# The first two matrices of a feed-forward layer: seven products of quarters in place of eight

## The chip, the cores and the metric

The kernel runs on one core of a Trainium2 chip. The metric is the time of one execution in device microseconds (us). Runs of the kernel before gave a median of 1726.57 us, from 1723.56 to 1729.68 (three runs).

## The reference

Two layers work on 256 context tokens and 256 latent tokens of width 1024. Layer 0 mixes with a recurrence and grouped attention and then runs a dense feed-forward layer (D_FF = 2816) over all 512 tokens; layer 1 mixes with a long convolution and latent attention and then runs a mixture of experts. The change lies in the dense feed-forward layer alone:

```python
def swiglu(h, w1, w3, w2):
    return (jax.nn.silu(h @ w1) * (h @ w3)) @ w2
...
def channel_mix(h):
    if even:
        return swiglu(h, ffn_w1[j], ffn_w3[j], ffn_w2[j])
    return moe_swiglu(h, moe_router[j], moe_w1[j], moe_w3[j], moe_w2[j])
...
xl = xl + mod_l[5] * channel_mix(modulate(rms_norm(xl, norm2_g[layer]), mod_l[3], mod_l[4]))
if need_ctx:
    xc = xc + mod_c[5] * channel_mix(modulate(rms_norm(xc, norm2_g[layer]), mod_c[3], mod_c[4]))
```

All of it is float32.

## The kernel before, in words

**Precision.** A float32 operand is held as two F32R tiles, `hi` (a rounded copy, by ScalarE) and `lo` (what the rounding left out, by a VectorE subtract). One product is `mm3` (L576): three matmuls, hi·hi, hi·lo and lo·hi, with a 128x128 piece of a weight stationary and the activations moving.

**Activations of the feed-forward layer.** The normed input stands transposed in eight tiles `h[k]`, each 128 channels by 512 tokens (tag `hhi`, `hlo`); columns 0 to 255 are the context, 256 to 511 the latents. `norm_pair` (L568) makes one `h[k]`: ACT writes hi, DVE writes lo, in two halves.

**Weights.** `Stream` (`ws`, L186 to L293) brings all weight matrices in their order of use: SP starts a DMA of 1 MB into one of two `raw` tiles (NR = 2), ACT copies it in two pieces of 128x1024 to `whi` (L260) and DVE subtracts to `wlo` (L273). `take()` gives the next block and splits one block ahead (LA = 1).

**The loops.** `FFN_PARTS` (L44) cuts the 22 column tiles of D_FF into parts of 8, 8 and 6. In a part, each iteration `b` (a "pair" below) does a w1 block and a w3 block of 256 columns: 2 blocks x 2 column tiles x 8 contraction tiles x 3 = 96 matmuls with 512 moving columns. ACT takes the silu from PSUM to `fs` (L1120), DVE multiplies by the w3 result (L1124), and `hilo` (L555 to L557) splits the product into `ah` (ACT) and `al` (DVE). Then four blocks of w2 (L1132 on) multiply the part's activations into the residual stream (`resid`, DVE, L1058). The first pair of the first part is different: each `h[k]` is made just ahead of its own matmuls.

```python
            else:
                bh, bl = take()
                p1 = [bank(), bank()]
                for m in range(2):
                    c = slice(m * 128, m * 128 + 128)
                    for k in range(KD):
                        mm3(p1[m], bh[:, k, c], bl[:, k, c], h[k][0], h[k][1], k == 0, k == KD - 1)
                bh, bl = take()
                p3 = bank2()
```

**Modulation.** `tick()` (L448) does one 128-row piece of the modulation matrices of a later stage: four small matmuls (L458) on a piece `rm` that came by DMA into a ring, here of 2 + 6 slots (L1054). Ticks are sprinkled through the loops; `tick_end` (L465) closes each eighth one.

**What sets the order.** From the norm to the end of the first pair the order on PE, DVE and ACT is the program's (`manual_schedule`, L1088 to `order.close()`, L1107). Elsewhere a scheduler orders each engine's instructions at build time from its own estimates; every engine then runs its list in that order. GpSimd (POOL) has no work in the feed-forward layer.

Of the kernel before, what the change touches and what calls it, by code (L numbers as in the profile page):

```python
# [138 lines left out]
def program(tc, a, out):  # L139
# [46 lines left out]
    class Stream:  # L186
# [389 lines left out]
    def mm3(p, wh, wl, xh, xl, first, last):  # L576
        TE.matmul(p, wh, xh, start=first, stop=False)  # L577
        TE.matmul(p, wh, xl, start=False, stop=False)  # L578
        TE.matmul(p, wl, xh, start=False, stop=last)  # L579
# [510 lines left out]
    pb = norm_last(0, 0, p, pn, (1, 3))  # L1090
    first = [take(0), take(0)]
    h = []
    for m0, mn in FFN_PARTS:
        act = []
        for b in range(mn // 2):
            if m0 + b == 0:
                p1, p3 = [bank(), bank()], bank2()
                h.append(norm_pair(pb, 0, 1, 0))
                for k in range(KD):
                    if k + 1 < KD:  # L1100
                        h.append(norm_pair(pb, 0, 1, k + 1))
# [4 lines left out]
                ws.split_to(ws.pos[2])
                order.close()  # L1107
            else:
                bh, bl = take()
                p1 = [bank(), bank()]  # L1110
                for m in range(2):
                    c = slice(m * 128, m * 128 + 128)
                    for k in range(KD):
                        mm3(p1[m], bh[:, k, c], bl[:, k, c], h[k][0], h[k][1], k == 0, k == KD - 1)
                bh, bl = take()
                p3 = bank2()
            for m in range(2):
                c = slice(m * 128, m * 128 + 128)
                s = ap.tile([128, T], F32, name=nm("fs"), tag="fs", bufs=2)
                A.activation(s, p1[m], AF.Silu)  # L1120
                if m0 + b:
                    for k in range(KD):
                        mm3(p3[:, m, :], bh[:, k, c], bl[:, k, c], h[k][0], h[k][1], k == 0, k == KD - 1)
                V.tensor_tensor(s, s, p3[:, m, :], op=OP.mult)  # L1124
                n = len(act) % 4
                if n == 0:
                    ah, al = wide("ah"), wide("al")
                hi, lo = ah[:, n, :], al[:, n, :]
                hilo(hi, lo, s)
                act.append((hi, lo))  # L1130
# [780 lines left out]
```

## Time and profile before

| what | value |
|---|---|
| median of 3 runs | 1726.57 us (1723.56 to 1729.68) |
| the profiled execution | 1723.7 us |
| its span in the profile | 1721.7 us |
| mean granted TensorE clock | 0.985 |
| PE busy | 1617.6 us (94%), 8369 matmuls |
| DVE, ACT, POOL busy | 767.6 (45%), 580.3 (34%), 113.0 us (7%) |
| HBM read over the span | 471.40 MB, 276 GB/s on average |

Times are microseconds from the start of the span. An engine is busy while it executes a matmul, a vector instruction and so on; issuing a DMA or waiting is not busy. Matmuls are pipelined, so what one shows as its own time (0.28 us and more) overlaps the next; the spacing of their starts is what a stream of them costs. A granted clock of 1.00 is TensorE's full 2.4 GHz, 0.50 is 1.2 GHz. "idle before <- X" is an engine's idle time ahead of an instruction and what ended it. The name of a tile is printed without its number.

### The profile page before, as it was taken

The page shows a single profiled execution, that of the slowest core. Times are in us where ns is not written, and L with a number is a line of the kernel's source. Part 1 is how long each engine was busy: PE and PEld are TensorE (multiplying, and loading weights), DVE is VectorE, ACT ScalarE, POOL GpSimd, SP SyncE. Part 2 cuts the span into 40 slices and gives each one's busy share as a digit, 9 for nine tenths or more (in the row PEclk, how much of TensorE's full clock was granted, in tenths as well). Part 3 has the DMA queues.
Part 4 walks back from the last instruction along what each step waited for, and adds up shares of the span by engine and source line. Part 5 has one row for each costly group of instructions (what it writes and reads, how often), then busy time and mean ns, then how long its engine had stood idle before and what let it go on. Part 6 is the DMA issues. An engine that isn't in the chain of part 4 may idle for free. (4 is left out here: it accounts for less than half of the span.)

```text
span 1721.7 us, 21415 instructions
## 1 busy us (share of the span) xinstructions
PE 1617.6 (94%) x8369; PEld 1025.8 (60%) x8369; DVE 767.6 (45%) x1214; ACT 580.3 (34%) x872; POOL 113.0 (7%) x81
## 2 busy tenths in 40 slices
PE   6898889999999999989999998999999999988886
PEld 2675666887777776776843434776446763423222
DVE  6679856334333326768630103884128852000001
ACT  3465743322222223554420103674136751000000
POOL 1433200000000000340000000000000000000000
PEclk9998999999999999999999999999999999999999
DMA  9534325223323333553799999999999989999997
GB/s 353 205 120 169 123 98 190 92 98 122 110 105 117 110 104 132 196 202 111 279 386 417 417 418 419 416 417 377 419 413 421 402 302 416 416 419 419 414 419 294
DMA packets 98989, 476.03 MB, mean 276 GB/s; under 512 B 8560, under 2 KB 34544, under 8 KB 53632
## 3 DMA queue, kind: packets, MB, share of 16 engines
q1 hardware_dynamic: 96256, 468.25, 69.3%
q0 software_dynamic: 1536, 5.28, 0.9%
q8 instruction: 68, 1.11, 0.3%
q10 hardware_dynamic: 1088, 1.05, 0.2%
q14 instruction: 41, 0.34, 0.1%
HBM read 471.40 MB, written 3.15 MB: 276 GB/s over the span
## 5 line engine op out<-in xcount | busy, mean ns | idle before, releaser
L273 DVE TENSOR_TENSOR wlo<-raw,whi 128x1024 fp32r<-128x1024 f32 (+2 forms) x240 | 282.1, 1209 | 201.4 <-ACT whi L260 193.9
L260 ACT ACTIVATE whi<-raw 128x1024 fp32r<-128x1024 f32 (+2 forms) x271 | 275.1, 1044 | 280.6 <-PE pm L578 115.7
L1736 PE MATMUL pm<-raw,xs 128*64 128x512 f32 (+1 forms) x1336 | 305.4, 551 | 23.2 <-DMA raw<-in_moe_w_dram 22.5
L1736 PEld LDWEIGHTS pm<-raw,xs 128*64 128x64 f32 x1336 | 103.7, 137 | 190.3 <-issue 138.0
L1855 DVE TENSOR_TENSOR es<-es,pm 128x512 f32<-128x512 f32 (+1 forms) x38 | 24.5, 644 | 339.6 <-PE pm L1736 328.5
L1736 PE MATMUL p<-raw,ats 128*64 128x512 f32 x616 | 152.2, 598 | 5.0 <-DMA raw<-in_moe_w_dram 4.3
L273 POOL TENSOR_TENSOR wlo<-raw,whi 128x1024 fp32r<-128x1024 f32 (+1 forms) x31 | 75.7, 2456 | 559.5 <-ACT k L1236 485.7
L1767 ACT ACTIVATE ats<-pm 128x512 f32<-128x512 f32 (+1 forms) x24 | 13.1, 544 | 285.1 <-PE p L1736 249.9
L577 PE MATMUL pm<-hhi,whi 128*128 128x512 f32 x240 | 96.4, 407 | 3.8 <-ACT hhi L565 3.8
L578 PE MATMUL pm<-hlo,whi 128*128 128x512 f32 x240 | 96.9, 404 | 1.0 <-DVE hlo L566 1.0
L1756 PE MATMUL pm<-wlo,xe 128*128 128x512 f32 x224 | 92.6, 414 | 4.0 <-DVE wlo L273 4.0
L579 PE MATMUL pm<-hhi,wlo 128*128 128x512 f32 x240 | 95.8, 400 | 0.0
L1736 PEld LDWEIGHTS p<-raw,ats 128*64 128x64 f32 x616 | 43.6, 136 | 86.8 <-issue 68.4
L1755 PE MATMUL pm<-whi,xe 128*128 128x512 f32 x224 | 88.0, 399 | 3.0 <-ACT whi L260 3.0
L577 PE MATMUL p<-hhi,whi 128*128 128x512 f32 x224 | 89.0, 398 | 1.3 <-ACT hhi L556 0.7
L578 PE MATMUL p<-hlo,whi 128*128 128x512 f32 x224 | 89.1, 398 | 0.0
L579 PE MATMUL p<-hhi,wlo 128*128 128x512 f32 x224 | 88.8, 396 | 0.0
L1848 ACT ACTIVATE es<-pm 128x512 f32<-128x512 f32 (+1 forms) x38 | 21.2, 559 | 156.2 <-PE pm L1736 150.7
L577 PE MATMUL pm<-ah,whi 128*128 128x512 f32 x176 | 70.2, 402 | 0.0
L458 PE MATMUL pm<-rm,sc 128*32 128x256 f32 x768 | 61.7, 408 | 8.8 <-DMA rm<-in_mod_w_dram 7.4
L578 PE MATMUL pm<-al,whi 128*128 128x512 f32 x176 | 69.6, 397 | 0.0
L579 PE MATMUL pm<-ah,wlo 128*128 128x512 f32 x176 | 69.0, 396 | 0.0
(454 smaller groups left out, 2678.6 us busy)
## 6 DMA issues: line engine op xcount, KB each, us to landing
raw<-in_moe_w_dram SPq DMA_DIRECT2D x300, 1024.0 KB, 15.2
rm<-in_mod_w_dram SPq DMA_DIRECT2D x96, 512.0 KB, 4.7
raw<-in_ffn_w_dram SPq DMA_DIRECT2D x30, 1024.0 KB, 4.8
xT<-in_moe_w_dram SPq DMA_DIRECT2D x24, 1024.0 KB, 18.4
raw<-in_ab_w_in_dram SPq DMA_DIRECT2D x7, 1024.0 KB, 6.6
raw<-in_cd_w_in_dram SPq DMA_DIRECT2D x6, 1024.0 KB, 6.5
whi<-in_moe_w_dram SPq DMA_DIRECT2D x12, 512.0 KB, 15.3
raw<-in_ab_w_out_dram SPq DMA_DIRECT2D x4, 1024.0 KB, 4.9
```

Source lines behind the costliest of these rows:

```text
L260: x = A.activation(h, c, AF.Copy)
L273: x = low.tensor_tensor(l, r, h.bitcast(F32), op=OP.subtract)
L458: TE.matmul(mst[2][32 * i:32 * i + 32, :256], sc[:, k, :], r[:, i * 256:(i + 1) * 256], start=k == 0, stop=k == 7)
L577: TE.matmul(p, wh, xh, start=first, stop=False)
L578: TE.matmul(p, wh, xl, start=False, stop=False)
L579: TE.matmul(p, wl, xh, start=False, stop=last)
L1736: TE.matmul(o if len(w.shape) == 2 else o.rearrange("p (a b) -> p a b", b=S), x, w, start=start, stop=stop)
L1755: TE.matmul(p, xh[:, k, :], bh[:, k, :], start=hf == 0 and k == 0, stop=False)
L1756: TE.matmul(p, xh[:, k, :], bl[:, k, :], start=False, stop=False)
L1767: A.activation(at[:, :n], p[:, :n * 128].rearrange("p (i s) -> p i s", i=n), AF.Copy)
L1848: A.activation(s[:, :w], p1[:, :w], AF.Silu)
L1855: V.tensor_tensor(s[:, :w], s[:, :w], p3[:, :w], op=OP.mult)
```

## The change

One level of Strassen's scheme replaces the products of w1 and w3 in all pairs but the first, 20 blocks in all. A block (1024 x 256) and the activations (1024 x 512) are cut in quarters: contraction tiles 0 to 3 and 4 to 7, two column tiles, context and latents. Seven products of a 512x128 quarter (or a sum or difference of two) with a 512x256 quarter (or a sum or difference) give what eight products give. Each has 4 contraction tiles x 3 matmuls, with 256 moving columns: 84 matmuls for a block in place of 48 of 512 columns. In detail:

- `quarters()` runs once, after the first pair. For each k of 0 to 3 it forms five sums or differences of quarters of `h`, each from three 128x256 additions (hi with hi, then each lo), then hi by ACT and lo by DVE (L1115). Three of them (products 1, 6, 7) are added by POOL and go to new tiles `h1`, `h6`, `h7`; two (3, 4) are added by DVE and overwrite a half of `h[k]`. That is 36 instructions of POOL, 24 + 20 of DVE, 20 of ACT.
- `Sevens.ahead(n)` makes the seven stationary operands of a block, five products ahead of their use. Five of the seven need a sum of weight quarters, a 128x512 addition on POOL (`sw`, three tiles, L1148); for all seven ACT writes `whi` (L1150) and DVE `wlo` (L1151), 128x512. The blocks are now wanted unsplit from `Stream`, so the L260 and L273 work on them goes.
- `Sevens.block(j)` runs the products 5, 2, 1, 3, 4, 6, 7 into four PSUM regions and combines them: two ACT copies (L1171, L1173), one POOL addition of 128x256 in SBUF (L1174), five DVE additions of 128x256 with one operand in PSUM (L1176 to L1181).
- Silu is taken and the multiplication done in halves of 256 columns.
- The modulation ring has 2 + 2 slots in place of 2 + 6, and the lookahead at the end of a part is handled apart (`take(0)`, `ahead(4)`).

The lines L1148 to L1181, L559, L580 to L582 and L460 are those of the changed file (L580 to L582 are the three matmuls of `mm3`, L577 to L579 before; L460 is the tick's matmul, L458 before; L566 and L568 are the norm's DVE lines, L564 and L566 before; L559 is L557 before). The core of the diff:

```diff
     NR, NH, LA = 2, 2, 1
+    RM, SW = 2, 3
...
-    mod_ring([(mq, "rm", 2)] * 2 + [(ap, "rm", 6)] * 6, 72)
+    mod_ring([(mq, "rm", 2)] * 2 + [(ap, "rm", RM)] * RM, 72)
...
+    def quarters():
+        for q in (1, 6, 7):
+            sums_q[q] = [ap.tile([128, 4, S], F32R, name=f"h{q}_{t}", tag=f"h{q}{t}", bufs=1) for t in ("hi", "lo")]
+        for k in range(4):
+            x, y = h[k], h[k + 4]
+            for q, (u, cu), (v, cv), op, E in ((1, (x, U0), (y, U1), OP.add, P), (6, (x, U0), (x, U1), OP.add, P),
+                                               (3, (x, U1), (y, U1), OP.subtract, V), (7, (y, U0), (y, U1), OP.add, P),
+                                               (4, (y, U0), (x, U0), OP.subtract, V)):
+                z = nw.tile([128, S], F32, name=nm("xn"), tag="xn", bufs=4)
+                E.tensor_tensor(z, u[0][:, cu].bitcast(F32), v[0][:, cv].bitcast(F32), op=op)
+                E.tensor_tensor(z, z, u[1][:, cu].bitcast(F32), op=OP.add)
+                E.tensor_tensor(z, z, v[1][:, cv].bitcast(F32), op=op)
+                hi, lo = [x[:, k, :] for x in sums_q[q]] if q in sums_q else [x[:, cu] for x in u]
+                A.activation(hi, z, AF.Copy)
+                V.tensor_tensor(lo, z, hi.bitcast(F32), op=OP.subtract)
+    MS = [(5, OP.add, (0, 0), (0, 1)), (2, OP.add, (1, 0), (1, 1)), (1, OP.add, (0, 0), (1, 1)), (3, None, (0, 0), None),
+          (4, None, (1, 1), None), (6, OP.subtract, (1, 0), (0, 0)), (7, OP.subtract, (0, 1), (1, 1))]
...
+                z = self.r[:, 4 * x[1]:4 * x[1] + 4, 128 * x[0]:128 * x[0] + 128]
+                if op:
+                    z2 = ap.tile([128, 4, 128], F32, name=nm("sw"), tag="sw", bufs=SW)
+                    P.tensor_tensor(z2, z, self.r[:, 4 * y[1]:4 * y[1] + 4, 128 * y[0]:128 * y[0] + 128], op=op)
+                    z = z2
+                A.activation(hi, z, AF.Copy)
+                V.tensor_tensor(lo, z, hi.bitcast(F32), op=OP.subtract)
...
+            for i, (q, *_) in enumerate(MS):
+                n0 = 7 * j + i
+                self.ahead(n0 + 5)
...
+                for k in range(4):
+                    mm3(dest[q], hi[:, k, :], lo[:, k, :], *met(q, k), k == 0 and q not in (3, 4, 7), k == 3, q in (3, 4, 7))
+                if q == 5:
+                    A.activation(d, pX, AF.Copy)
+                if q == 2:
+                    A.activation(s2, pY, AF.Copy)
+                    P.tensor_tensor(d, d, s2, op=OP.add)
+                if q == 1:
+                    V.tensor_tensor(t, pZ, d, op=OP.subtract)
+                if q == 6:
+                    V.tensor_tensor(t, t, pW, op=OP.add)
+                    V.tensor_tensor(t, t, pX, op=OP.add)
+            V.tensor_tensor(e, pZ, d, op=OP.subtract)
+            V.tensor_tensor(e, e, pY, op=OP.add)
+            return [[e, pX], [pY, t]]
...
+                j = 2 * (b - (m0 == 0))
+                fs = [ap.tile([128, T], F32, name=nm("fs"), tag="fs", bufs=2) for _ in range(2)]
+                for m, x in enumerate(sevens.block(j)):
+                    for c, u in zip(x, (U0, U1)):
+                        A.activation(fs[m][:, u], c, AF.Silu)
+                for m, x in enumerate(sevens.block(j + 1)):
+                    for c, u in zip(x, (U0, U1)):
+                        V.tensor_tensor(fs[m][:, u], fs[m][:, u], c, op=OP.mult)
+                    activations(fs[m])
```

How the lists of the engines change is shown at three places. First PE, at the end of the first pair. Before, the next w1 block follows with 512 columns (`pm_2701`):

```order
L577 MATMUL p_437_2485<-hhi_2628,ah_2376 128x512
L578 MATMUL p_437_2485<-hlo_2629,ah_2376 128x512
L579 MATMUL p_437_2485<-hhi_2628,al_2377 128x512
L577 MATMUL pm_2701<-hhi_2486,whi_2662 128x512
L578 MATMUL pm_2701<-hlo_2487,whi_2662 128x512
L579 MATMUL pm_2701<-hhi_2486,wlo_2664 128x512
```

Now, after product 5 (`p_500`, the latents of `h[4]` to `h[7]`), the products 1 and 6 (`pm_2820`, `pm_2821`) stand with the sums `h_hi`, `h_lo` of `quarters()`, and ticks behind them:

```order
L582 MATMUL p_500_2819<-hhi_2620,wlo_2794 128x256
L580 MATMUL pm_2820<-h_hi,whi_2803 128x256
L581 MATMUL pm_2820<-h_lo,whi_2803 128x256
L582 MATMUL pm_2820<-h_hi,wlo_2804 128x256
L580 MATMUL pm_2821<-h_hi,whi_2826 128x256
L581 MATMUL pm_2821<-h_lo,whi_2826 128x256
L582 MATMUL pm_2821<-h_hi,wlo_2827 128x256
L460 MATMUL pm_3732<-rm_2815,sc 32x256 x4
L460 MATMUL pm_3732<-rm_3099,sc 32x256 x4
```

Twelve matmuls of the next block need no sum; after them PE needs the first sums, and 16 ticks that stood throughout the layer now stand between here and the end of the second block.

Second POOL, from the last work of the mixer before the layer. Before, layer 1's weights come next:

```order
L885 TENSOR_TENSOR hlo_1952<-u,hhi_1951 128x512
L273 TENSOR_TENSOR wlo_5169<-raw_5043,whi_5167 128x1024
L273 TENSOR_TENSOR wlo_5170<-raw_5043,whi_5168 128x1024
```

Now the sums of weights (`sw`) and of activations (`xn`) stand there, the first of them:

```order
L1148 TENSOR_TENSOR sw_2882<-raw_2376 128x512
L1110 TENSOR_TENSOR xn_2673<-hhi_2478,hhi_2554 128x256
L1148 TENSOR_TENSOR sw_2900<-raw_2376 128x512
L1110 TENSOR_TENSOR xn_2679<-hhi_2478 128x256
L1111 TENSOR_TENSOR xn_2673<-xn_2673,hlo_2479 128x256
L1110 TENSOR_TENSOR xn_2691<-hhi_2554 128x256
```

All but one of the 36 sums of activations stand behind `sw_2900`, which takes one of three `sw` tiles, free once the DVE subtract of an earlier one is done; that subtract (`wlo_2827<-sw_2843`) stands in DVE's list among the last four subtracts of the norm.

Third DVE, in the second pair. Before, it has the two subtracts for each block, the multiplications and the activations' subtracts:

```order
L273 TENSOR_TENSOR wlo_2753<-raw_2697,whi_2751 128x1024
L273 TENSOR_TENSOR wlo_2754<-raw_2697,whi_2752 128x1024
L1124 TENSOR_TENSOR fs_2762<-fs_2762,p_492_2761 128x512
L557 TENSOR_TENSOR al_2675<-fs_2762,ah_2674 128x512
L273 TENSOR_TENSOR wlo_2828<-raw_2699,whi_2826 128x1024
```

Now the subtracts of 128x512 alternate with the combinations of products, which read PSUM:

```order
L1151 TENSOR_TENSOR wlo_3183<-sw_3184,whi_3182 128x512
L1151 TENSOR_TENSOR wlo_3183<-sw_3200,whi_3182 128x512
L1176 TENSOR_TENSOR dd_3108<-pm_3104,dd_3106 128x256
L1178 TENSOR_TENSOR dd_3108<-dd_3108,pm_3105 128x256
L1151 TENSOR_TENSOR wlo_3219<-raw_3002,whi_3218 128x512 x2
L1179 TENSOR_TENSOR dd_3108<-dd_3108,p_543_3103 128x256
L1151 TENSOR_TENSOR wlo_3263<-sw_3264,whi_3262 128x512
L1151 TENSOR_TENSOR wlo_3263<-sw_3282,whi_3262 128x512
L1180 TENSOR_TENSOR dd_3109<-pm_3104,dd_3106 128x256
```

In all, PE's list goes from 9403 to 10120 rows, DVE's from 2058 to 2321, POOL's from 113 to 269; SP's keeps 1501.

## Rows read from the trace of the kernel before

**Rows 1.** The page: the engines' busy time; the granted clock in 40 slices of the span.

```profile
PE 1617.6 (94%) x8369; PEld 1025.8 (60%) x8369; DVE 767.6 (45%) x1214; ACT 580.3 (34%) x872; POOL 113.0 (7%) x81
...
PEclk9998999999999999999999999999999999999999
```

**Rows 2.** Windows: us; PE, PEld, DVE, ACT, POOL busy; granted clock; DMA share; GB/s.

```profile
291.10:316.80 25.70, 25.67 (x124) 18.91 (x123) 16.16 (x35) 12.37 (x21) 0.00 (x0) 1.00 0.60 230
316.80:384.10 67.30, 67.30 (x289) 54.11 (x288) 22.40 (x25) 17.96 (x24) 0.00 (x0) 1.00 0.26 94
384.10:678.00 293.90, 293.90 (x1325) 228.00 (x1324) 104.26 (x141) 75.21 (x92) 0.00 (x0) 1.00 0.33 115
678.00:693.00 15.00, 12.09 (x87) 8.02 (x86) 12.59 (x33) 6.28 (x15) 0.00 (x0) 0.77 0.22 72
860.00:1721.70 861.70, 810.48 (x3845) 411.07 (x3845) 281.44 (x347) 237.46 (x300) 5.09 (x4) 0.99 0.99 401
```

**Rows 3.** Waits from 291 to 678 us: us in total, times, longest.

```profile
PE pm L469 <- ACT stg L466: 0.7, 1, 0.7
...
DVE wlo L273 <- ACT whi L260: 141.3, 48, 8.0
```

**Rows 4.** Timeline of PE early in the kernel: start, us; matmuls of 256 columns.

```profile
100.53 0.28 PE L578 MATMUL p<-wlo,hhi 128*128 128x256 f32 x1
...
101.13 0.28 PE L577 MATMUL p<-whi,hhi 128*128 128x256 f32 x1
```

**Rows 5.** Groups by form: busy us, mean ns of one, idle before; the whole span.

```profile
L273 DVE TENSOR_TENSOR wlo<-raw,whi 128x1024 fp32r<-128x1024 f32 x228 | 270.6, 1221 | 190.8 <-ACT whi L260 189.6 <-PE pm L1758 1.0
L273 POOL TENSOR_TENSOR wlo<-raw,whi 128x1024 fp32r<-128x1024 f32 x29 | 72.1, 2498 | 554.4 <-ACT k L1236 485.7 <-ACT whi L260 68.7
L1058 DVE SCALAR_TENSOR_TENSOR xT<-pm,modc,xT 128x256 f32<-128x256 f32 x56 | 24.7, 479 | 50.1 <-PE pm L579 50.1
L557 DVE TENSOR_TENSOR al<-fs,ah 128x512 fp32r<-128x512 f32 x22 | 15.1, 689 | 7.2 <-ACT ah L556 7.1
L556 ACT ACTIVATE ah<-fs 128x512 fp32r<-128x512 f32 x22 | 13.8, 628 | 47.0 <-DVE fs L1124 46.9
L885 POOL TENSOR_TENSOR hlo<-u,hhi 128x512 fp32r<-128x512 f32 x4 | 5.1, 1289 | 1.2 <-ACT hhi L884 1.1
```

**Rows 6.** Timelines of DVE and POOL at moments when both work.

```profile
23.86 3.44 DVE L489 TENSOR_TENSOR sa<-sa,sq 128x512 f32<-128x512 f32 x2
24.09 2.66 POOL L637 TENSOR_TENSOR fs<-fil 128x1024 f32<-128x1024 f32 x1 [1.88 <-DVE fil L622]
...
66.05 2.61 DVE L566 SCALAR_TENSOR_TENSOR hlo<-xn,modc,hhi 128x256 fp32r<-128x256 f32 x1
65.62 2.77 POOL L273 TENSOR_TENSOR wlo<-raw,whi 128x1024 fp32r<-128x1024 f32 x1 [5.59 <-ACT whi L260]
...
145.63 3.36 DVE L785 TENSOR_TENSOR t<-t,row 128x1024 f32<-128x1024 f32 x1
145.55 2.35 POOL L273 TENSOR_TENSOR wlo<-raw,whi 128x1024 fp32r<-128x1024 f32 x1
147.86 2.26 POOL L882 TENSOR_TENSOR u<-u,gate 128x512 f32<-128x512 f32 x1
...
198.90 0.68 DVE L557 TENSOR_TENSOR hlo<-pm,hhi 128x512 fp32r<-128x512 f32 x1
198.79 2.41 POOL L864 TENSOR_TENSOR lw<-lw,lw 128x1024 f32<-128x1024 f32 x1
```

**Rows 7.** Timeline of DVE: the norm's last subtracts, then two activations' subtracts.

```profile
304.16 0.89 DVE L566 SCALAR_TENSOR_TENSOR hlo<-xn,modc,hhi 128x256 fp32r<-128x256 f32 x2 [0.18 <-ACT hhi L565]
...
319.03 1.29 DVE L557 TENSOR_TENSOR al<-fs,ah 128x512 fp32r<-128x512 f32 x2
```

**Rows 8.** Groups of PE from 384.1 to 678 us: the ticks.

```profile
L458 PE MATMUL pm<-rm,sc 128*32 128x256 f32 x118 | 10.0, 390 | 0.0
```

**Rows 9.** The page, DMA issues: KB each, median us from issue to landing.

```profile
raw<-in_ffn_w_dram SPq DMA_DIRECT2D x30, 1024.0 KB, 4.8
```

More of the change, by code (lines that the diff above doesn't have):

```diff
@@ L315, in program @@
         for b in range(mn // 2):
-            want(*colblk('ffn_w1', (m0 + 2 * b) * 128, 256))
-            want(*colblk('ffn_w3', (m0 + 2 * b) * 128, 256))
+            for w in ('ffn_w1', 'ffn_w3'):
+                src, cols, _, shape = colblk(w, (m0 + 2 * b) * 128, 256)
+                want(src, cols, m0 + b == 0, shape)
         for c0 in range(0, 1024, 256):
@@ L574, in norm_pair, with mm3 @@
         return hi, lo
[L576 to L579, printed above, removed]
+    def mm3(p, wh, wl, xh, xl, first, last, more=False):
+        TE.matmul(p, wh, xh, start=first, stop=False, skip_group_check=more)
+        TE.matmul(p, wh, xl, start=False, stop=False, skip_group_check=more)
+        TE.matmul(p, wl, xh, start=False, stop=last, skip_group_check=more)
     def norm_full():
@@ L1092, in program @@
     h = []
+    U0, U1 = slice(0, S), slice(S, T)
+    sums_q = {}
+    def quarters():
[13 more added lines that the diff above has]
+                V.tensor_tensor(lo, z, hi.bitcast(F32), op=OP.subtract)
@@ L1093, in program, with activations @@
+    sevens = None
     for m0, mn in FFN_PARTS:
         act = []
+        def activations(s):
+            n = len(act) % 4
+            if n == 0:
+                whole[:] = wide("ah"), wide("al")
+            hi, lo = [x[:, n, :] for x in whole]
+            hilo(hi, lo, s)
+            act.append((hi, lo))
+        whole = []
         for b in range(mn // 2):
@@ L1105, in program @@
                             mm3(pq[m], bh[:, k, c], bl[:, k, c], h[k][0], h[k][1], k == 0, k == KD - 1)
-                ws.split_to(ws.pos[2])
                 order.close()
-            else:
[L1109 to L1130, printed above, removed]
+                for m in range(2):
+                    s = ap.tile([128, T], F32, name=nm("fs"), tag="fs", bufs=2)
+                    A.activation(s, p1[m], AF.Silu)
+                    V.tensor_tensor(s, s, p3[:, m, :], op=OP.mult)
+                    activations(s)
@@ new lines, in program @@
+                sevens = Sevens(mn - 2)
+                quarters()
+                sevens.ahead(4)
+            else:
+                j = 2 * (b - (m0 == 0))
[7 more added lines that the diff above has]
+                    activations(fs[m])
@@ L1131, in program @@
             tick()
         for b in range(4):
-            bh, bl = take()
+            bh, bl = take(0 if b == 3 and m0 < 16 else None)
+            if b == 3 and m0 < 16:
+                sevens = Sevens(FFN_PARTS[m0 // 8 + 1][1])
+                sevens.ahead(4)
             for m in range(2):
```

31 lines of the change are left out of this document (added).

## The prediction

> **What bounds the kernel now.** I read the page first: PE is busy for 94% of the span and its clock is granted in full nearly everywhere [rows 1]. Then windows by stage [rows 2]. The first pair ends at 316.8 us; the three other pairs of part 0 fill the 67.3 us to 384.1, with PE busy in all of it: 288 matmuls, so 67.3 / 288 = 0.2336 us for one of 512 columns. From there to the layer's last matmul at 678.0 us PE is busy without a gap too; its only wait is one of 0.7 us, while DVE waits 141 us for ACT, which itself runs after PE [rows 3]. So in this layer PE alone sets the pace, DVE is busy for a third of it and POOL does nothing at all [rows 2]. After 860 us DMA is at 0.99 [rows 2]: the experts' weights set the end there. What the layer's end gains or loses passes on in full, because those loads go into memory that the program frees at points behind this layer; I see no slack that would swallow a shift.
>
> **PE's own part.** The change takes 20 blocks x 48 = 960 matmuls of 512 columns out, 960 x 0.2336 = 224.3 us, and puts in 20 x 84 = 1680 of 256 columns. Their price: five in a row between 100.53 and 101.13 us, 0.12 each [rows 4]; half of 0.2336 would be 0.117, and I take 0.118: 198.2 us. So PE's work falls by 26.0 us. A pair (w1 block and w3 block) goes from 96 x 0.2336 = 22.4 us to 168 x 0.118 = 19.8. The Trainium skill ("TensorE: Matmul & The Clock Gate", the section on the issue gap of back-to-back matmuls) gives N/2.4 GHz plus about 2.5 ns; an estimate by it is 207.2 against 183.4 us, a gain of 23.8 in place of 26.0. The rows' spacing is longer at both sizes, and I keep the rows.
>
> **What goes from ACT and DVE.** The splits of 128x1024 go (DVE 1.22 us each [rows 5], two per block), and seven of 128x512 per block come. In bytes this is 7/4 of the work: 14 x 0.69 = 9.7 us per pair on DVE [rows 5] in place of 4.9; ACT 14 x 0.63 = 8.8, plus copies, silu and hi about 4.5, so 13 us of 19.8. ACT is hidden. The weights' DMA lands in 4.8 us [rows 9] against 10 us per block, and a raw tile is free again a block ahead: hidden. SP has the same number of entries. Silu and multiplication in halves add about 1 us per pair to ACT and DVE, hidden beside PE.
>
> **What POOL and DVE do to each other** is the heart of it. Per pair POOL gets 10 weight sums of 128x512 and 2 additions of 128x256. A POOL addition of 128x512 took 1.29 us [rows 5]. But look at the moments when both engines work [rows 6]. At 24.09 POOL runs 2.66 us, to 26.75; two DVE additions of 128x512 with both operands in SBUF, begun at 23.86, end only at 27.30, the second 0.55 after POOL. At 66.05 a DVE subtract of 128x256, 0.48 otherwise, takes 2.61 and ends 0.27 after POOL's (65.62 + 2.77 = 68.39). At 145.63 it is DVE that holds POOL too: DVE's 128x1024 waits for POOL's first (ends 147.90), then ends at 148.99, and POOL's 128x512 ends at 150.12, 1.13 after it. So an SBUF-SBUF addition on DVE and one on POOL go one after the other: they cost 0.55 (512 columns) or 0.27 (256) of DVE, and 1.13 of POOL; for 256 columns on POOL, 1.13 less half of (2.35 - 1.13 = 1.2 per 512), about 0.55 to 0.60, and I take 0.60. Against this, the DVE subtract of 198.90 with one operand in PSUM took 0.68 beside a POOL instruction of 2.41: not held up.
>
> Per pair that makes, in turn: POOL 10 x 1.13 + 2 x 0.60 = 12.5; DVE 14 weight subtracts and 2 of the activations, 16 x 0.55 = 8.8 (the four halves' multiplications and the combinations have an operand in PSUM, 12 to 14 x 0.35 to 0.48, and run beside POOL). Sum 21.3, and about 1.2 for turns in which one hands over late: **22.5 us**, over PE's 19.8 and beside 22.4 before. So in a steady pair the exchange gives nothing: the gain of PE becomes a wait for the stationary operands. The Trainium skill speaks against such a use of POOL ("SBUF — State Buffer", "Who interferes with whom"): a DVE instruction with two SBUF inputs contends with a GpSimd one that reads SBUF, one with at most one SBUF input doesn't. The traced moments agree on both (2.61 and 0.68 us). The skill's measured 4497 ns for 2048 columns ("GPSIMD Engine Reference", section 3.1) would make a 512 about 1.12, an estimate, and the sum the same. At the row's 1.29 [rows 5] a pair would be 24.
>
> **The start: sums of activations.** POOL's sums stand behind a weight sum that is free after DVE's last norm subtracts, which end at about 305 [rows 7]. In turn then: POOL 35 x 0.60 + 5 weight sums x 1.13 + 2 x 0.60 = 27.9; DVE 24 + 20 of 256 columns x 0.27 and 10 subtracts x 0.55 = 17.4. 304 + 45.3 = 349. PE finishes the first pair at 316.8 [rows 2], has 12 matmuls and 16 ticks without sums (64 x 0.085 = 5.4 us [rows 8]) and then gets on with each k as it comes; behind the last sums some 80 matmuls are left, 9.5 us, a little of them done sooner: the second pair ends at about 357. Without a stall it would end at 316.8 + 19.8 + 5.4 = 342; the stall is 15 us.
>
> **The sum, on the profiled execution.** Two pairs after 357 at 22.5: part 0's pairs end at 402 (before 384.1). Before, 384.1 to 678.0 holds 1200 matmuls x 0.2336 = 280.3 and 13.6 of ticks and gaps. Now: w2 528 x 0.2336 = 123.3; part 1, four pairs, 90 less 4 that POOL and DVE have done ahead during w2: 86; part 2, three pairs, 67.5 - 4.5 = 63; ticks and gaps 13.6 - 5.4 - 2.5 (fewer) = 5.5. 402 + 277.8 = 679.8, against 678.0: +1.8, and about 1 more because PE, when it idles near 320 to 350, may drop to half clock for a few us, as it does after its gaps at 686 (0.77 over 678 to 693 [rows 2]). So +3 us: 1723.7 + 3 = 1726.7 for the profiled execution; that execution is 2.9 below the median, so **1729.5** in terms of the runs. Own range: 1722 to 1738, from the stall (10 to 20), the turns (22 to 23.3 per pair).
>
> **Rivals.** *Turns are hidden* (chance 0.20): if POOL and DVE interleave better than instruction by instruction, pairs go at 19.8: part 0 5.4 less, parts 1 and 2 6.8 and 3.6 less, 16 us: 1713. For it: PE may run up to five products behind the preparation. Against it: all three moments of [rows 6] show full exclusion. *No exclusion at all, stall small* (0.06): -26 and +3 for the start: 1706. Only 198.90 speaks for it. *DVE's combinations wait as well* (0.26; the slower side): the place is DVE's list, where the combinations stand between two weight subtracts. DVE runs in order; a subtract that waits for POOL holds the PSUM additions behind it, and POOL has gone on to its next sum when they are done. Then a pair costs 12.5 + 8.8 + 4.5 = 25.8, with half of it hidden 24.6; and PE, whose next blocks need these PSUM regions, waits too. It decides as soon as a pair passes 22.8. Nine pairs x 2.2 to 3.3: 20 to 30 us, 1750 to 1760, I name 1752. For it: the order of the list; against it: 198.90. *The change doesn't do what it says*: all the named instructions stand in the lists, so nothing for that. The half clock as a rival: were the whole stall at half clock and the first 100 matmuls after it too, 100 x 0.118 = 12 us more, 1741; that lies within the range and gets no chance of its own.
>
> **How the numbers follow.** Forecast 0.48, the three rivals 0.20, 0.06, 0.26. A change of 0.3%, 5.2 us, is about what a measurement can tell. Of the forecast's 0.48 (its centre +3, its range -4 to +9 and a tail) 0.06 falls to faster, 0.26 to no change, 0.16 to slower; of the first rival all is faster but 0.02, of the last all slower but 0.01. Faster 0.30, same 0.29, slower 0.41. The range from 1709 to 1755 leaves out the case without exclusion (0.06) and the upper ends.
>
> **What would show it.** Right: POOL busy for 150 us and more between 290 and 680; L1151's subtracts well over 0.69 us on the mean, many over 1.5, as each waits for a POOL sum; the matmuls of 256 columns 0.118 apart; between 317 and 350 PE waiting for DVE's L1115 (`h_lo`); pairs of 22 to 23 us in which PE waits for L1151; the last matmul of the layer near 680. Wrong: pairs of 20 us, or L1151 at 0.7 beside POOL (the exclusion is weaker), or pairs over 24 with PE waiting for the combinations (L1176 to L1181), or a span whose difference does not come from this layer at all.

## The result and the profile after

The changed kernel takes 1755.12 us (median of 4 runs, 1754.04 to 1757.44) against 1725.07 for the kernel before on the same chip: ratio 1.017, 95% interval 1.0148 to 1.0193. It is 30 us slower. The forecast named 1729.5, with an own range of 1722 to 1738 and a widest range up to 1755: the time lies 0.1 us past the upper end of the wide one and 17 past the own one. The direction was right, the size was not.

The page of the changed kernel's profiled execution (1757.44 us, span 1755.7), the rows that answer to [rows 1]:

```profile
PE 1613.5 (92%) x9089; PEld 1059.1 (60%) x9089; DVE 929.9 (53%) x1478; ACT 643.8 (37%) x1054; POOL 313.1 (18%) x237
...
POOL 1433201872562460152000000000000000000000
PEclk9898999899989999899999999999999999999999
```

Windows by stage, columns as in [rows 2] (the first pair; the other pairs of part 0; the pairs of part 1; of part 2; the 24 us behind the layer's last matmul):

```profile
291.10:321.50 30.40, 26.82 (x131) 20.09 (x132) 22.89 (x45) 11.39 (x24) 9.83 (x11) 0.94 0.45 162
321.50:415.10 93.60, 78.89 (x653) 66.62 (x652) 83.48 (x125) 44.49 (x93) 63.86 (x55) 0.95 0.46 160
460.10:553.40 93.30, 85.92 (x673) 84.36 (x673) 77.38 (x108) 45.74 (x91) 57.14 (x42) 0.95 0.27 93
598.40:665.90 67.50, 61.46 (x505) 60.03 (x504) 56.24 (x81) 33.45 (x67) 40.92 (x30) 1.00 0.26 91
699.70:724.00 24.30, 18.23 (x108) 12.54 (x107) 16.37 (x38) 9.93 (x20) 0.00 (x0) 0.72 0.39 130
```

The accounts, in starts of matmuls of the two profiles: the first pair ends at 321.5 in place of 316.8 (+4.7). The three pairs behind it take 93.6 us in place of 67.3 (+26.3). From there w2 of part 0 takes 45.1 to the next part's first matmul, before 46.4 (-1.3). Part 1, from its first matmul to part 2's first, takes 138.3, before 141.1 (-2.8); part 2 to the layer's last matmul 101.0, before 106.0 (-5.0). So the layer ends at 699.4, not 677.6: +21.8. The next layer's first matmul comes at 712.6, before at 685.6 (+27.0), the experts' first at 910.5 against 879.1 (+31.4), and the spans differ by 34.0. The small gain of parts 1 and 2 is far from the 26 us that PE's work fell by, and the start of part 0 takes more than all of it.

The groups of POOL and DVE from 290 to 720 us, by form (mean ns of one behind the busy time), answering to [rows 5]:

```profile
L1148 POOL TENSOR_TENSOR sw<-raw 128x512 f32<-128x512 f32 x94 | 146.0, 1567 | 137.4 <-DVE wlo L1151 82.1 <-DMA raw<-in_ffn_w_dram 53.2 <-DVE gm L425 2.0
L1151 DVE TENSOR_TENSOR wlo<-sw,whi 128x512 fp32r<-128x512 f32 x97 | 83.9, 895 | 13.2 <-ACT whi L1150 13.2
L1151 DVE TENSOR_TENSOR wlo<-raw,whi 128x512 fp32r<-128x512 f32 x39 | 43.5, 1120 | 5.3 <-ACT whi L1150 5.3
L559 DVE TENSOR_TENSOR al<-fs,ah 128x512 fp32r<-128x512 f32 x22 | 22.7, 1057 | 0.6 <-ACT ah L558 0.3
L1225 DVE TENSOR_TENSOR fs<-fs,dd 128x256 f32<-128x256 f32 x20 | 18.0, 898 | 0.0
L1176 DVE TENSOR_TENSOR dd<-pm,dd 128x256 f32<-128x256 f32 x20 | 8.4, 418 | 15.7 <-POOL dd L1174 15.7
L1225 DVE TENSOR_TENSOR fs<-fs,p 128x256 f32<-128x256 f32 x20 | 7.4, 408 | 0.0
```

Everything on DVE with both operands in SBUF is longer than its 0.69 (512 columns) by 0.2 to 0.4 us on the mean; the same multiplication L1225 takes 0.898 with an operand in `dd` (SBUF) and 0.408 with one in PSUM. The combinations, which read PSUM, take 0.42. So far the exclusion is as forecast. The Trainium skill ("SBUF — State Buffer", "Who interferes with whom") makes just this difference between two SBUF inputs and one; the two rows of L1225 agree.

Two pairs of part 1, on POOL's timeline, the same point in each:

```profile
486.80 3.09 POOL L1148 TENSOR_TENSOR sw<-raw 128x512 f32<-128x512 f32 x2 [1.96 <-DVE wlo L1151]
...
511.34 3.08 POOL L1148 TENSOR_TENSOR sw<-raw 128x512 f32<-128x512 f32 x2 [1.95 <-DVE wlo L1151]
```

A pair in the middle of a part takes 24.5 us, not 22.5 (the same point comes again at 536.77, 25.4 us later). PE's waits from 290 to 720 us, in us, times, longest:

```profile
PE pm L580 <- ACT whi L1150: 9.5, 7, 1.7
PE pm L460 <- DMA rm<-in_mod_w_dram: 7.8, 6, 2.5
PE p L582 <- DVE wlo L1151: 4.2, 6, 0.8
PE pm L582 <- DVE wlo L1151: 3.9, 6, 1.1
PE p L580 <- ACT hhi L1114: 3.8, 2, 3.2
...
PE pm L580 <- DVE dd L1176: 0.2, 1, 0.2
```

PE waits for stationary operands (`whi`, `wlo`), as forecast, and hardly for the combinations (the last row). The second row was not forecast: ticks that wait for their pieces. Its worst place is the norm ahead of the first pair. Timelines of PE, ACT and DVE there:

```profile
292.18 0.64 PE L460 MATMUL pm<-rm,sc 128*32 128x256 f32 x8 [1.46 <-DMA rm<-in_mod_w_dram]
295.32 0.64 PE L460 MATMUL pm<-rm,sc 128*32 128x256 f32 x8 [2.50 <-DMA rm<-in_mod_w_dram]
...
302.13 0.39 ACT L468 ACTIVATE stg<-pm 128x256 f32<-128x256 f32 x1 [5.24 <-PE pm L460]
302.41 0.90 ACT L567 ACTIVATE hhi<-xn,modc 128x256 fp32r<-128x256 f32 x2
...
302.95 0.48 DVE L568 SCALAR_TENSOR_TENSOR hlo<-xn,modc,hhi 128x256 fp32r<-128x256 f32 x1 [4.75 <-ACT hhi L567]
```

With four ring slots in place of eight, the eighth tick can run only late; the ACT copy that closes the eight ticks (L468) stands in ACT's list among the norm's `hhi`, waits 5.24 us for them, and holds the norm. DVE's last norm subtract ends at 315.0, before at 305.0 [rows 7]. The ring is about half of these 10 us, the 4.75 that DVE waits. The norm's first subtract comes 2.4 later too (292.81, before 290.44), and the last ones stand among subtracts of weights and beside POOL's first sums; two of the norm's multiplications take 2.39 us there, 0.87 elsewhere in this norm:

```profile
311.30 2.39 DVE L566 SCALAR_TENSOR_TENSOR xn<-xT,gm,rs 128x256 f32<-128x256 f32 x2
```

Behind the layer the same happens on PE:

```profile
705.95 0.64 PE L460 MATMUL pm<-rm,sc 128*32 128x256 f32 x8 [0.78 <-DMA rm<-in_mod_w_dram]
708.91 1.08 PE L460 MATMUL pm<-rm,sc 128*32 128x256 f32 x8 [2.33 <-DMA rm<-in_mod_w_dram]
```

and the granted clock of that stretch is 0.72 on the mean, before 0.77 over a shorter one [rows 2].

### The profile page after: what moved, and what is told of

It is laid out like the page before. It is cut to its first block, busy times and chain, and to the rows that moved or that the text cites. A ratio compares the mean times of both kernels' runs of the same rounds, so it can differ in the third digit from the quotient of the medians.

```text
span 1755.7 us, 23607 instructions
## 1 busy us (share of the span) xinstructions
PE 1613.5 (92%) x9089; PEld 1059.1 (60%) x9089; DVE 929.9 (53%) x1478; ACT 643.8 (37%) x1054; POOL 313.1 (18%) x237
## 5 line engine op out<-in xcount | busy, mean ns | idle before, releaser
L261 ACT ACTIVATE whi<-raw 128x1024 fp32r<-128x1024 f32 (+2 forms) x231 | 232.7, 1042 | 146.0 <-PE pm L581 55.6
L274 DVE TENSOR_TENSOR wlo<-raw,whi 128x1024 fp32r<-128x1024 f32 (+2 forms) x200 | 235.0, 1215 | 71.9 <-ACT whi L261 70.6
L1954 DVE TENSOR_TENSOR es<-es,pm 128x512 f32<-128x512 f32 (+1 forms) x38 | 24.5, 644 | 340.6 <-PE pm L1835 329.5
L1148 POOL TENSOR_TENSOR sw<-raw 128x512 f32<-128x512 f32 x100 | 154.3, 1558 | 196.2 <-DMA raw<-in_ffn_w_dram 109.9
L580 PE MATMUL p<-hhi,whi 128*128 128x256 f32 (+1 forms) x384 | 118.2, 309 | 7.9 <-ACT hhi L1114 3.8
L582 PE MATMUL p<-hhi,wlo 128*128 128x256 f32 (+1 forms) x384 | 117.4, 306 | 4.2 <-DVE wlo L1151 4.2
L581 PE MATMUL p<-hlo,whi 128*128 128x256 f32 (+1 forms) x384 | 117.1, 305 | 0.0
L1151 DVE TENSOR_TENSOR wlo<-sw,whi 128x512 fp32r<-128x512 f32 x100 | 86.3, 893 | 13.4 <-ACT whi L1150 13.4
L1150 ACT ACTIVATE whi<-sw 128x512 fp32r<-128x512 f32 x100 | 59.8, 626 | 69.6 <-PE pm L581 27.8
L460 PE MATMUL pm<-rm,sc 128*32 128x256 f32 x768 | 64.8, 431 | 20.8 <-DMA rm<-in_mod_w_dram 20.2
L580 PEld LDWEIGHTS p<-hhi,whi 128*128 128x128 f32 x384 | 74.3, 194 | 13.7 <-ACT hhi L1114 4.8
L582 PEld LDWEIGHTS p<-hhi,wlo 128*128 128x128 f32 x384 | 74.3, 193 | 8.2 <-DVE wlo L1151 5.4
L580 PE MATMUL pm<-h_hi,whi 128*128 128x256 f32 x240 | 69.3, 291 | 9.9 <-ACT whi L1150 9.5
```

The costliest lines, as they stand in the source:

```text
L261: x = A.activation(h, c, AF.Copy)
L274: x = low.tensor_tensor(l, r, h.bitcast(F32), op=OP.subtract)
L460: TE.matmul(mst[2][32 * i:32 * i + 32, :256], sc[:, k, :], r[:, i * 256:(i + 1) * 256], start=k == 0, stop=k == 7)
L580: TE.matmul(p, wh, xh, start=first, stop=False, skip_group_check=more)
L581: TE.matmul(p, wh, xl, start=False, stop=False, skip_group_check=more)
L582: TE.matmul(p, wl, xh, start=False, stop=last, skip_group_check=more)
```

## The experiments

Each run also has a measured ratio to the kernel before on its chip. Stages are compared in the profiles by two lengths: **part 1**, from its first matmul to part 2's first (four pairs, w2, and eight ticks where they are kept there; PE's work alone is 672 x 0.118 + 192 x 0.2336 = 124.2), and **the start**, from the first pair's last matmul to the 168th product matmul recorded behind it, about the end of the second pair. In the changed kernel they are 138.3 and 45.2 us (321.2 to 366.4).

### The ring (e1_ring)

```diff
-    mod_ring([(mq, "rm", 2)] * 2 + [(ap, "rm", RM)] * RM, 72)
+    mod_ring([(mq, "rm", 2)] * 2 + [(ap, "rm", RM)] * RM + [(ap, t, 1) for t in ("h1hi", "h1lo", "h6hi", "h6lo")], 48)
-    pb = norm_last(0, 0, p, pn, (1, 3))
+    pb = norm_last(0, 0, p, pn, (1, 7))
                 order.close()
+                mod_ring([(mq, "rm", 2)] * 2 + [(ap, "rm", RM)] * RM, 72)
+                if 48 <= j < 72:
+                    tc.keep_in_program_order(x)
```

> The changed kernel, with eight modulation pieces again in the ring while the norm runs (four of them in the tiles of the activations' sums, which are not yet in use), eight ticks there in place of four, and the ticks of the layer kept at their places in the program. In the changed kernel PE waits for a piece inside the first pair (1.5 and 2.5 us, then half clock) and twice behind the layer (0.8 and 2.3 us, then half clock), and the distance to the kernel before grows from 22 us at the layer's last matmul to 32 us some 60 us later. Theory (the shorter ring costs about 10 us, apart from the products): the first pair ends 2 to 3 us sooner, and that later growth goes; 1744, within 4. Rival (the ring's waits stand in the shadow of other waits): 1755, within 3.

Measured: 1748.53 us, ratio 1.0136 (1.011 to 1.0161), 6.6 less. The first pair ends at 317.1 (changed 321.5), DVE's last norm subtract at 311.3 (before 305.0, changed 315.0), the second pair at 362.7 (changed 366.4), and from the layer's last matmul to the next layer's first it is 8.2 us (before 8.0, changed 13.2). But the layer itself ends at 704.2, 4.8 later than the changed kernel's: its ticks now stand in the parts (part 1: 141.7), where in the changed kernel 16 of them ran in the start's wait. What brings the time down lies behind it: from the next layer's first matmul to the experts' first it takes 189.8 us, changed 197.9. PE's waits for pieces in that stretch, first in the changed kernel, then here:

```profile
PE pm L460 <- DMA rm<-in_mod_w_dram: 9.1, 6, 2.8
...
PE pm L460 <- DMA rm<-in_mod_w_dram: 4.1, 3, 2.0
```

The ring's waits are real; what they cost in all is less than I expected, since the short ring had also put ticks where PE was idle.

### No weight sums (e2_no_weight_sums)

```diff
-                if op:
-                    z2 = ap.tile([128, 4, 128], F32, name=nm("sw"), tag="sw", bufs=SW)
-                    P.tensor_tensor(z2, z, self.r[...], op=op)
-                    z = z2
```

> The sums of weight quarters are left out: the five products use one quarter each, ACT's and DVE's splits stay. Theory (POOL's sums and DVE's SBUF subtracts exclude each other, and that sets a pair): without them DVE has some 17 us per pair, the subtracts of 128x512 take 0.65 to 0.7 on the mean, pairs of parts 1 and 2 go at PE's pace, 19.8 to 20.3 us in place of 22.5 to 23.3; part 1's stretch 80 to 82 us (93.2 before), in all about 1730. Rival (the combinations of the products in PSUM, or ACT, set the pair): 22 us and more remain.

Measured: part 1 takes 124.7 us, and PE is busy in all of it. The subtracts, 136 of them, take 0.72, the multiplication with `dd` 0.423. Windows of part 1's and part 2's pairs, and the subtracts:

```profile
448.60:528.80 80.20, 80.20 (x676) 80.07 (x675) 59.19 (x112) 45.25 (x91) 7.94 (x8) 1.00 0.33 113
573.20:633.20 60.00, 60.00 (x508) 59.87 (x507) 42.85 (x82) 32.98 (x67) 5.87 (x6) 1.00 0.32 107
...
L1147 DVE TENSOR_TENSOR wlo<-raw,whi 128x512 fp32r<-128x512 f32 x136 | 92.9, 720 | 36.4 <-ACT whi L1146 36.1
```

A pair is 20.0 us. The seven products run at PE's pace as soon as POOL's sums are gone: neither ACT nor the combinations bound them. (The single total of 1716.78 is not compared: the experts' work depends on their input.)

### All on DVE (e3_dve)

```diff
-                    P.tensor_tensor(z2, z, self.r[:, ...], op=op)
+                    V.tensor_tensor(z2, z, self.r[:, ...], op=op)
-            for q, (u, cu), (v, cv), op, E in ((1, (x, U0), (y, U1), OP.add, P), ...
+            for q, (u, cu), (v, cv), op, E in ((1, (x, U0), (y, U1), OP.add, V), ...
-                    P.tensor_tensor(d, d, s2, op=OP.add)
+                    V.tensor_tensor(d, d, s2, op=OP.add)
```

> All that POOL does in the layer goes to DVE (weight sums, activations' sums, the addition of two PSUM copies): DVE gets 12 instructions more per pair. Theory (exclusion): in turn the two took 23 us; DVE alone needs 24 x 0.60 + 2 x 0.65 + about 1.5 + 4.6 = 21.8, so a pair takes 21.8 to 22.3 although the busiest engine has 7 us more of work; the start is shorter by 8 to 15 us, because 80 instructions of 0.33 take 27 us in place of 45 in turns; in all 1735, within 6. Rival (no exclusion, DVE bound by its own list or by hand-overs over three tiles): a pair takes 26 us and more, and the time goes to 1775 and above.

Measured: 1731.69, ratio 1.0036 (1.0021 to 1.0052): 23 us less than the changed kernel with nothing left out. Part 1 takes 127.7, a pair 20.7, less than the 21.8 that I gave it at least. Its groups:

```profile
L1151 DVE TENSOR_TENSOR wlo<-sw,whi 128x512 fp32r<-128x512 f32 x97 | 65.0, 687 | 12.2 <-ACT whi L1150 12.2
L1148 DVE TENSOR_TENSOR sw<-raw 128x512 f32<-128x512 f32 x94 | 63.2, 687 | 1.0 <-DMA raw<-in_ffn_w_dram 1.0
L1225 DVE TENSOR_TENSOR fs<-fs,dd 128x256 f32<-128x256 f32 x20 | 8.4, 422 | 0.3
```

The busiest engine got more work and the pairs became shorter: 94 sums cost DVE 63 us here, and had cost POOL 146. That is exclusion, not a lack of DVE. The start, though, did not shorten: its last subtract ends at 361.1 (changed 361.8), against my 8 to 15 us less. DVE begins the sums at 313.1. The 80 instructions do take 27 us (they start 0.335 apart), but DVE's other work among them (sums and subtracts of weights, the first pair's multiplications, combinations), which I had left out, takes some 14, and for 6.8 us DVE waits for others, most of it at two places:

```profile
350.70 0.24 DVE L475 TENSOR_TENSOR modc<-pm,par 128x8 f32<-128x8 f32 x2 [2.72 <-PE pm L471]
...
358.09 0.42 DVE L1178 TENSOR_TENSOR dd<-dd,pm 128x256 f32<-128x256 f32 x1 [2.79 <-PE pm L582]
```

The first closes eight ticks, the second combines a product. So this run shows the exclusion in the pairs, not in the start.

### No sums of activations (e4_no_act_sums)

The call of `quarters()` is left out, and products 1, 6, 7, 3, 4 take halves of h as they are.

> The sums of activation quarters are left out (products 1, 6, 7, 3, 4 use halves of h as they are). Theory (the sums hold PE for 25 to 30 us behind the first pair): the three pairs of part 0 take 63 to 70 us in place of 93.6, parts 1 and 2 stay as they are, in all about 1728. Rival (the stall comes from the weights' side, or from the ticks that were moved there): part 0's pairs still take over 80 us.

Measured: the start takes 22.9 us in place of 45.2, part 0's pairs 68.5 (321.1 to 389.6) in place of 93.6, with PE busy throughout; part 1 takes 137.8, six ticks among it. Seven of the 18 ticks that the changed kernel has in part 0 stand later here (4.6 us), so the sums of activations hold part 0 by some 20 us, and the weights' side is apart from it. The ticks don't hold the start: in e1 it is as long (45.9) with one tick in it as in the changed kernel with 16. (Its total of 2914 us is not comparable: all of the excess lies behind 889 us, with the experts.)

### Fewer sums, all on DVE, long ring (e5_full_dve), and POOL's share (e6_two_pool, e7_three_pool)

```diff
+            f = {}
+            for w in (x, y):
+                f[id(w)] = nw.tile([128, T], F32, name=nm("sq"), tag="sq", bufs=3)
+                V.tensor_tensor(f[id(w)], w[0].bitcast(F32), w[1].bitcast(F32), op=OP.add)
-                E.tensor_tensor(z, u[0][:, cu].bitcast(F32), v[0][:, cv].bitcast(F32), op=op)
-                E.tensor_tensor(z, z, u[1][:, cu].bitcast(F32), op=OP.add)
-                E.tensor_tensor(z, z, v[1][:, cv].bitcast(F32), op=op)
+                V.tensor_tensor(z, f[id(u)][:, cu], f[id(v)][:, cv], op=op)
-                    A.activation(s2, pY, AF.Copy)
-                    P.tensor_tensor(d, d, s2, op=OP.add)
+                    V.tensor_tensor(d, pY, d, op=OP.add)
-                    P.tensor_tensor(z2, z, self.r[:, ...], op=op)
+                    (P if q in () else V).tensor_tensor(z2, z, self.r[:, ...], op=op)
-                quarters()
                 sevens.ahead(4)
+                quarters()
```

with the ring's edit of e1; in the other two `()` is `(5, 6)` and `(5, 1, 7)`.

> All sums on DVE, and fewer: hi + lo of the two tiles of h once for each k (two additions of 128x512), then one addition of 128x256 for each of the five sums in place of three; the weights' first products come ahead of them; the copy s2 and the addition of two copies become one DVE addition from PSUM; ring and ticks as in the run on the ring. Theory (exclusion, the start's sums, and the ring are the three losses): DVE needs 18 us in place of 27 for the start's sums, the second pair ends near 345 us, pairs of parts 1 and 2 take 20.5 us, the growth behind the layer is gone; 1714, within 8, so 0.3 to 1% faster than the kernel before. Rival (the seven products cost PE something besides their columns, clock or hand-overs, that no placing of the sums removes): 1725 and above.

> As the run with all sums on DVE, but POOL makes two of the five weight sums of a block (products 5 and 6). Theory (what counts is the sum of POOL's and of DVE's SBUF work): 4 x 1.13 + 20 x 0.60 + 2 x 0.60 + 0.7 = 18.4 us in turns, DVE in all 18.6: below PE's 19.8, so pairs take 19.9 to 20.2, 0.3 to 0.6 less than with all on DVE; in all 2 to 5 us less. Rival (POOL's share costs in hand-overs what it saves on DVE): the same or slower by 5.

> As before it, with three of the five weight sums on POOL (products 5, 1, 7). Theory: 6 x 1.13 + 18 x 0.60 + 1.2 + 0.7 = 19.5 in turns, just below PE's 19.8: pairs 20 to 20.5, about as with two; the turns end the gain. Rival (exclusion costs less than full turns here): faster than with two by 2 us and more.

Measured: 1711.11, ratio 0.992 (0.9903 to 0.9936); with two sums on POOL 1721.71 (0.9952 to 0.9979), with three 1723.35 (0.9971 to 0.9997). The first is faster than the kernel before: the start takes 31.7 us, two ticks in it (the second pair ends at 349.8, not at 345), part 1 130.8, which less eight ticks of 0.68 is 125.4, within 1.2 of PE's work. With PE at its own pace there was nothing left for POOL to save: part 1 takes 131.7 and 134.1. Against e5, e6 is 10.6 us slower, more than its rival had. POOL's 16 sums of part 1 take 1.97 us each in e6 and DVE's sums there 0.77 in place of 0.68, so I was wrong that sharing gains 2 to 5 us. A part of what e6 and e7 lose (9 and 6 us) lies between the next layer's first matmul and the experts' first (199.6 and 196.9 us against 190.7), where the three kernels have the same work in slightly different order; its cause was not traced.

### Four tiles for the weight sums (e8_four_sw)

```diff
-    RM, SW = 2, 3
+    RM, SW = 2, 4
-            d, s2, t, e = [ap.tile(...) for i in range(4)]
+            d, t = [ap.tile(...) for i in (0, 2)]
+            s2, e = nw.tile([128, S], F32, name=nm("xn"), tag="xn", bufs=4), d
```

> The changed kernel with four tiles for the weight sums in place of three (the combination e takes d's tile, and s2 a tile of the norm's, to make room). POOL waits 82 us in the layer for DVE to free one of the three. Theory (POOL and DVE work in turn; the wait is the other side of the same turns): pairs of part 1 stay at 23 to 23.5 us, in all within 4 of 1755. Rival (three tiles are too few: the hand-over from POOL over ACT to DVE and back sets the pair): pairs of 21 to 22, in all 1740 or less.

Measured: 1751.78, ratio 1.0143 (1.0113 to 1.0174); part 1 136.8, so 0.4 us per pair less. POOL still waits 73 us for DVE. The wait on three tiles is not the cause.

### Two plain pairs (e9_two_plain)

In the kernel of e5 the second pair, too, is done with eight products, and `quarters()` comes behind it.

> As the run with all sums on DVE and fewer of them, but the second pair is done with eight products too, so that the sums of activations are made beside it. It gives back 2.6 us of PE's gain. Theory (the start still costs that run about 7 us of idle PE and half clock between 317 and 345 us): the wait goes, net 2 to 5 us faster than it: 1708. Rival (the sums for products 3 and 4, which overwrite halves of h and so come after the second pair, hold the third as long): 1711 to 1718.

Measured: 1713.16, ratio 0.993 (0.9906 to 0.9954), no gain on e5 (1711.11): the rival.

### One edit each, and both (e10_start_only, e11_weights_only, e12_both)

e10 is the changed kernel with `f`, as in e5's diff, and the order of `ahead(4)` and `quarters()`; e11 is it with `V` in place of `P` in the weight sums; e12 has both. Ring, ticks and POOL's addition L1174 are the changed kernel's in all three.

> The changed kernel with one edit: the sums of activations on DVE, from hi + lo added once (8 additions of 128x512 and 20 of 128x256 in place of 60 of 128x256), behind the weights' first products; the weight sums stay on POOL. Theory (start and pairs are separate losses): part 0's three pairs end 12 to 20 us sooner after the first, the pairs of parts 1 and 2 stay at 22.5 to 23.5; 1740, within 5. Rival (the start is held by the weights or by ticks): under 6 us.

> The changed kernel with one edit: the weight sums on DVE, the activations' sums as they are on POOL and DVE. Theory: pairs of parts 1 and 2 at 20.3 to 20.6 us, 17 to 20 us less for the seven; part 0 changes by less than 8; 1737, within 5. Rival (turns matter only while both are full): pairs above 21.5.

> The changed kernel with the two edits of the last runs together: the activations' sums on DVE from hi + lo, and the weight sums on DVE; the ring and the ticks as in the changed kernel. Theory (three separate losses): 1755.1 - 13.7 - 25.0 = 1716.4, within 4; what is left to the run with the long ring (1711.1) is the ring's part, 3 to 9 us. Rival (both edits shorten the same wait, or the ring's waits only come out when the others are there): 1724 and above, or below 1711.

Measured: e10 1741.43 (ratio 1.0059 to 1.0119), e11 1730.08 (1.0001 to 1.0029), **e12 1709.55, ratio 0.9906 (0.9888 to 0.9924)**, the lowest, though its interval overlaps that of e5. In e10 part 0's pairs end 16 us sooner after the first and part 1 stays at 136.3 (two ticks in it); in e11 part 1 takes 125.8, and DVE waits only 3.8 us for POOL's addition in place of 15.7. e10 came as expected; e11 gained more (25 us in place of 18) and lies below its range. Together they save 45.6 us, 7 more than the two apart, and e12 lies below the range of its theory; but by the ratios it is 5 us more, less than the four intervals can tell, so that the two losses simply add up is neither shown nor refuted. e12 in windows (first pair; other pairs of part 0; parts 1 and 2 with the first of w2; behind the layer):

```profile
293.20:320.50 27.30, 27.05 (x122) 20.37 (x119) 19.55 (x49) 11.16 (x25) 0.00 (x0) 0.88 0.36 131
320.50:397.70 77.20, 76.16 (x667) 67.28 (x666) 69.46 (x142) 43.14 (x88) 12.23 (x6) 1.00 0.56 205
438.70:523.90 85.20, 84.66 (x691) 83.18 (x690) 77.10 (x145) 45.52 (x91) 11.23 (x8) 1.00 0.31 111
564.60:627.20 62.60, 62.30 (x515) 61.63 (x515) 55.90 (x105) 33.06 (x67) 8.88 (x6) 1.00 0.30 102
658.80:682.00 23.20, 17.77 (x127) 11.87 (x126) 16.38 (x38) 9.90 (x19) 0.00 (x0) 0.85 0.42 137
```

PE is busy for 99% of the pairs. The layer ends at 658.5 us, 19 sooner than before and 8 sooner than in e5: the ticks that the scheduler put behind the first pair run while PE would wait. It gives back 4 us behind the layer (12.1 us to the next layer's first matmul against 8.1 in e5) and 7 up to the experts. That the ring costs 3 to 9 us in e12 as well was wrong as a total. That its two effects (waits, and ticks put where PE is idle) nearly cancel is my reading; e5 and e12 differ in the addition of the two copies too, so it isn't shown.

## Why the prediction was right or wrong

- **PE's part: right.** 0.118 for 256 columns carries every stage in which PE is never idle (part 1 of e2: 124.7 against 124.2 worked out).
- **Exclusion of POOL and DVE: right**, shown for the pairs by e2, e3 and e11. Taking POOL's weight sums away brings a pair from 23.3 to 20.2 us (e11), though DVE then does them.
- **The pair of 22.5 us: too cheap.** A pair in the middle takes 24.5; with what is prepared during w2 the four pairs of part 1 take 93.3 where I had 86, the three of part 2 67.5 where I had 63. The lead of 4 us at a part's start was right. Two items were mis-sized. I put all four multiplications down as reading PSUM; half of them have `e` or `t` in SBUF and are held (0.898 against 0.408). And the prices were those of tight turns. In the pair from 486.80 one of the two engines is at an instruction on SBUF operands for 23.0 of the 24.5 us, where I had 21.3, so their turns fill nearly all of it. Four lines of that pair and the next:

```profile
498.29 5.15 POOL L1148 TENSOR_TENSOR sw<-raw 128x512 f32<-128x512 f32 x3
...
523.80 2.56 POOL L1148 TENSOR_TENSOR sw<-raw 128x512 f32<-128x512 f32 x2
...
490.96 1.28 DVE L1151 TENSOR_TENSOR wlo<-sw,whi 128x512 fp32r<-128x512 f32 x2
...
494.09 0.42 DVE L1176 TENSOR_TENSOR dd<-pm,dd 128x256 f32<-128x256 f32 x1 [1.86 <-POOL dd L1174]
```

  Where the two alternate, an addition and a subtract take 1.72 us together (5.15 for three), near my 1.13 + 0.55. Where one goes twice on end, POOL's costs 1.27 (2.56 less the 1.29 of one alone) and DVE's 0.60 (1.28 less 0.68). An estimate with these, 0.72 for POOL's addition of two copies and 0.33 for the two multiplications: 10 x 1.27 + 2 x 0.72 + 16 x 0.60 + 2 x 0.33 = 24.4 if no turn were tight. The 23.0 lie between that and my sum for tight turns; the other 1.5 us pass with DVE's work on PSUM while POOL waits. So the allowance of 1.2 us was too small. One place where they are not is DVE's list: DVE waits up to 1.9 us at a time, 15.7 in the layer, for POOL's addition of the two copies, which stands behind weight sums in POOL's list. The clock doesn't set the pair: with the 4 us done ahead counted in, a pair of part 2, where the granted clock is 1.00, takes 23.8 us, and one of part 1, at 0.95, 24.3.
- **The third rival: near in number, in part by luck.** Its 24.6 doesn't follow from its own sum (25.8 less half of 4.5 is 23.6, or 24.8 with the 1.2 for late turns), its mechanism came in part only: DVE's list does stop with the combinations behind it, but they run in 0.42 and PE waits 0.2 us for them. And its 1750 to 1760 was to come from pairs slower by 20 to 30 us; they were slower by 15.5 (4 + 7 + 4.5), and the rest came from the late start and from behind the layer, which stand in no rival.
- **The start: length right, beginning wrong.** I had 45 us of turns from 304; measured 47 us from 315.0 (the norm's last subtract; POOL's first sum came at 309.1) to 361.8. The second pair ended at 366, not 357, and the two behind it took 49 us, not 45. The 10 us by which the norm was late is the step that failed. About half of it is the shorter ring, which stood in the diff and which I gave no cost at all, though ACT's copy for the ticks stands among the norm's writes: DVE waits 4.75 us, and with the long ring (e1) the second pair ends 3.7 sooner. In e1 the norm still ends 6 us later than before, so the rest isn't the ring's: the subtracts of weights and POOL's sums, which stand among the norm's last instructions, stretch its end, and of the 2.4 us by which it begins late the cause stays open.
- **Behind the layer: not in the sum.** I let the end pass on 1:1 from the last matmul; it grew by 5 us there, where ticks wait for the ring, by 4 to the experts' first matmul and by 2.6 to the end. The first two are the ring's with its ticks: e1 has 8.2 us up to the next layer's first matmul and 189.8 from there to the experts' first (changed 13.2 and 197.9). The last is open.
- **Ticks: mis-sized.** The trace has two records for each tick matmul, so 16 ticks are 128 records and 10.9 us, not 5.4. Because they fell into PE's wait, the later parts were 5 us shorter than I had them.
- **The sum of it** at the layer's last matmul: 9 (start) + 4 (rest of part 0) + 7 + 4.5 (pairs) - 5 (ticks) = 19.5; I had 679.8, measured 699.4. Two slips in the prediction's sums change little: 13.6 - 5.4 - 2.5 is 5.7, not 5.5, and 1726.6 - 26 + 3 is 1703.6, not 1706.

Open: why the next layer takes 190 us in e1 and e5, 193.5 before and 194 to 205 in the others. In the changed kernel the waits for the ring's pieces are 5 of the 8 us over e1; in e12, with 198, PE waits only 2.0 us for them. Not tried: e12's ticks with a longer ring at the end of the layer.

## What to carry to other kernels

Before giving an idle GpSimd elementwise work, add its time to that of VectorE's instructions with two SBUF operands, because that sum, not the larger of the two, is what the stage needs; here 94 sums cost 146 us on POOL, held VectorE besides, and cost 63 us on VectorE. A cheaper product needs its operands faster: count the preparation per block against the new matmul time, and save additions (hi + lo once in place of three sums) before moving them. And a buffer that is made smaller to make room is part of the change: look for the instruction on another engine that stands behind it in order.

## What was not expected of the hardware

POOL's and DVE's turns also hold POOL: a 128x512 addition took 1.57 us on the mean among DVE's work, 1.97 with only four per pair (e6), against 1.29 [rows 5]. The Trainium skill says "use DVE for elementwise" stays the rule ("GPSIMD Engine Reference", section 3.1), for the speed of the engine alone, with a ratio of 1.96 for an addition of 2048 columns. Here 1.29 against 0.69 us is 1.9, and for the 94 sums, 146.0 on POOL among DVE's work (changed) against 63.2 on DVE (e3), it is 2.3, and DVE is held besides. And waits of 0.8 to 3.2 us on PE were followed by stretches at half clock (a granted clock of 0.72 on the mean over the 24 us behind the layer, 0.77 from 340 to 355), which the second pair paid on top of the wait itself.
